# Fourteen elementwise shares and nineteen weight splits taken from GpSimd and given to VectorE

## The chip, the core and the metric

The kernel runs on one core of a Trainium2 chip. A core has TensorE for matrix products, VectorE, ScalarE and GpSimd for elementwise work, and SyncE, whose queue issues nearly all of this kernel's transfers between HBM and the core's memories SBUF and PSUM. The metric is the device time of one execution in microseconds (us); lower is better.

## The reference, cut to what matters

A token sequence of 256 rows and 1024 columns in float32 runs through three layers. Each layer begins with an RMS norm, a wide input product, a mixer and an output product; the first two layers also have an MLP with a squared ReLU.

```python
x = x + rmsnorm(even_mixer(rmsnorm(x, g[0]), ...), g[1])      # layer 0
x = x + rmsnorm(sq_relu_mlp(rmsnorm(x, g[2]), w1, w2), g[3])
...                                                           # layer 1: odd_mixer and a second MLP
h = rmsnorm_2(x, norm_g) * (1 + scale) + shift                # layer 2: scale, shift and gate from silu(c) @ w_ada + b_ada
merged = sigmoid(m_attn) * y_attn + sigmoid(m_conv) * y_conv
return rmsnorm_2(x + gate * (merged @ w_out), final_g)
```

`even_mixer` joins a gated linear recurrence over 4 heads (`hgrn2_scan`, its output normed per head, times a learned gain, times `silu(hgate)`) and a retention over 4 heads whose queries and keys are turned by `rope`, `x1 * cos - x2 * sin` and `x2 * cos + x1 * sin`. `odd_mixer` is an mLSTM behind a short convolution. Layer 2 joins causal attention with a bias by distance and a gated short convolution.

## The kernel before, in words

All weights are read once from HBM, 512 KB at a time, into one of five `raw` buffers (`RB`). TensorE multiplies in a format with fewer bits than float32, so each such unit is split into two parts that add up to it: ScalarE copies `raw` into the high part (`A`, L261), and a subtraction makes the low part from `raw` and the high part. Both lie in one of eight `u` buffers (`NU`). Each product then takes three passes: high by high, low by high and high by low. The activations are split in the same way: `to_act` transposes a normed row on TensorE, ScalarE copies the high part out of PSUM, VectorE subtracts for the low part. The operations are written through small helpers: `tt` is an elementwise operation on two tensors (L265 in the profile), `stt` one with a scalar between (L276), `A` one of ScalarE (L261), `mm` a product (L292), `tr` a transpose (L296).

The instruction streams of the engines are ordered when the program is built. `Sched` keeps an estimate of when each engine is through with what it was given, by a cost for each instruction and the tiles it reads and writes; `sc.E["p"]` (also `sc.t`) is TensorE's estimate, `"v"`, `"a"` and `"g"` are those of VectorE, ScalarE and GpSimd. The products of weights are a list `prog` of steps, each with a cost, and so each weight unit has a time at which it is due. After each product `sc.run` resumes side jobs (norm chains, scans, gates, which are generators) whose estimated time has come, and then calls `pump`. `pump` issues loads as long as a `raw` buffer is free, and splits units ahead of need, up to eight. A unit that is due within `LEAD` (7000 ns) is split as soon as its load is nearly there. One that is due later waits, if its load isn't there, if ScalarE is over 800 ns ahead of TensorE, or if the earlier of VectorE and GpSimd (GpSimd with 1100 ns on top) is over 500 ns ahead. `need` splits whatever a product needs at once. Each engine then executes its stream in the order that resulted, and semaphores make it wait for what it reads or overwrites.

In `emit_split` (L375) the low part goes to GpSimd where its estimated end there is 200 ns (`POOL_BIAS`) or more ahead of that on VectorE:

```python
fv, fg = max(sc.E["v"], hi_t) + 1137.0, max(sc.E["g"], hi_t) + 2220.0
tt(u[:, 1, :], t, u[:, 0, :].bitcast(F32), ALU.subtract, "g" if fg < fv + POOL_BIAS else "v")
```

Three more places give `tt` the engine `"g"`, GpSimd:

- `post` (L570) ends a norm chain. For each half of the 128 rows' columns VectorE multiplies the product by the row's scale and a gain, and `x` is added to: the first half on GpSimd, the second on VectorE. `pre` then takes the squares of both halves on ScalarE, VectorE scales, and `to_act` transposes and splits.
- `rope_evac` (L859): three products on VectorE, then their sum on GpSimd; TensorE transposes the sum.
- `ev_first` (L702): the gate `silu(hgate)` times the learned gain `ghg`, the same for all rows. `ghg` is loaded by `small_loads` (L665), which is called in the same step, one after the scan's `masks`.

GpSimd also does memsets. The blocks `stagA` and `out_stag` take the 256 tokens in two halves of 128, so that the norm chain of one half can run beside the products of the other; `blockA` and `blockB` take all tokens together. Between one output product and the next input product lies a norm chain; such places are called transitions below. While `hgrn` (the scan of layer 0) runs as a side job, TensorE multiplies for the retention.

Of the kernel before, what the change touches and what calls it, by code (L numbers as in the profile page):

```python
# [10 lines left out]
F32 = mybir.dt.float32  # L11
# [3 lines left out]
ALU = mybir.AluOpType  # L15
# [16 lines left out]
LEAD = 7000.0  # L32
POOL_BIAS = -200.0

# [13 lines left out]
class Sched:  # L48
    """Orders the instruction streams. It keeps an estimate of when each engine is through
    with what it was given and when each part of a tile was last written and read, and  # L50
    resumes side jobs (generators) when what they issued last should have finished."""

# [70 lines left out]
    def reuse(self, tag, bufs, ap):  # L123
        """A new tile in the place of the bufs-th last one of its tag."""
        ring = self.ring.setdefault(tag, [])
        ring.append(ap)
        if len(ring) > bufs:
            old = ring.pop(0).tensor.name
            acc = self.W.get(old, []) + self.R.get(old, [])
            self.W[ap.tensor.name] = [(0, 1 << 20, t, w) for l, h, t, w in acc]  # L130
# [39 lines left out]
class Act:  # L170
    """An activation, split into two float32r parts that add up to it exactly,
    features on partitions; lay 'tk': [128, 2, K, 128], 'kt': [128, K, 256]."""

# [30 lines left out]
def tile_model(ctx: ExitStack, tc: tile.TileContext, I: dict, out: bass.AP, stop=None):  # L204
# [36 lines left out]

    # ---------------------------------------------------------- instructions
    def fs(ap):
# [57 lines left out]
    def bc(ap2, n):  # L301
        """[128, m] -> [128, n, m], the same for each of n."""
        return ap2[:, None, :].to_broadcast([ap2.shape[0], n, ap2.shape[1]])
# [4 lines left out]

    # ------------------------------------------------------------ constants
    x = cpool.tile([128, 2, D], F32, name="x")  # L310
# [26 lines left out]

    # ----------------------------------------------------- streams of weights
    units = []
# [35 lines left out]
    def emit_split():  # L375
        k = st["split"]
        kind, val = order[k]
        t = raws.pop(k)
        if kind == "w":
            u = pool.tile([128, 2, 1024], F32R, tag="u", bufs=NU, name=nm("u_"))  # L380
            if len(st["free"]) >= st["nu"] - NU + 1 > 0:
                sc.W[u.tensor.name] = [(0, 2048, st["free"][st["nu"] - NU], "p")]
            st["nu"] += 1
            A(u[:, 0, :], t)
            hi_t = sc.E["a"] + sc.OTHER
            fv, fg = max(sc.E["v"], hi_t) + 1137.0, max(sc.E["g"], hi_t) + 2220.0
            tt(u[:, 1, :], t, u[:, 0, :].bitcast(F32), ALU.subtract, "g" if fg < fv + POOL_BIAS else "v")
            tiles[val] = u
            st["live"] += 1
        else:  # L390
            val[1](t)
        st["done"].append(max(sc.E["v"], sc.E["a"] + 1300.0))
        st["split"] += 1

    def pump():
        while True:
# [8 lines left out]
            if order[k][0] == "w" and due[order[k][1]] - st["at"] > LEAD:  # L405
                if st["arrive"][k] > sc.t + 300 or sc.E["a"] > sc.t + 800 or \
                        min(sc.E["v"], sc.E["g"] + 1100.0) > sc.t + 500:
                    return
# [34 lines left out]

    # ------------------------------------------------------ weight products
    def mmA(ps, act, T, kt, u, off, start, stop_):
# [18 lines left out]
    def blockA(w, c0, act, evac, alloc=None):  # L464
        """512 columns, tokens on partitions; evac({T: bank})."""
        us = units1(w, c0)
# [14 lines left out]
    def stagA(wcs, act, evac, before=None):  # L481
        """Two blocks of 512 columns: both for one half of the tokens, then both for the other."""
        us = [units1(w, c) for w, c in wcs]
# [17 lines left out]
    def blockB(w, c0, act, evac, alloc=None, nk=8):  # L501
        """512 columns as four groups of 128 partitions, tokens along the row; evac([bank, bank])."""
        us = units1(w, c0, 0, nk)
# [14 lines left out]

    # ------------------------------------------------------------ norm chains
    def junk():  # L520
        return pool.tile([128, 512], F32, tag="junk", bufs=1, name=nm("junk_"))

    class Stat:
        """Sum of squares over a row of 1024 in two halves, and 1/sqrt(mean + eps)."""

# [16 lines left out]
    def to_act(src, act, T, k0, n):  # L542
        """src [128 tokens, n*128] -> its transpose in act (k0.. of half T)."""
        pt = axb()
# [25 lines left out]
    def post(T, st_, yb, g):  # L570
        """x += rmsnorm(y) * g; the first half of y is in st_ already."""
        rs = st_.second(yb[1])
        for h in range(2):
            c = slice(h * 512, h * 512 + 512)
            t = s2()
            stt(t, yb[h], rs, g[:, c], ALU.mult, ALU.mult)
            tt(x[:, T, c], x[:, T, c], t, ALU.add, "g" if h == 0 else "v")
        yield
# [6 lines left out]
    class Stage:  # L585
        """Jobs that bring h for one stage, half by half."""

# [12 lines left out]
    def row_order(n):  # L600
        """(half of the columns, unit): unit by unit, but the last ones by halves of the columns,
        so that the first half is there early."""
        return ([(h, j) for j in range(n - TAIL) for h in range(2)]
                + [(h, j) for h in range(2) for j in range(n - TAIL, n)])

    def out_stag(us, act_of, nxt, gpost, gpre, shift=None, ybanks=None, first=True):
        """The last eight rows-units of an out-product: half T of the tokens at a time,
        the norms of one half under the products of the other."""
        n = len(us)
# [22 lines left out]

    # =============================================================== layer 0
    w_ev = I["ev_w_in"][0]
# [3 lines left out]
    def setup():  # L638
# [5 lines left out]
        for h in range(2):  # L644
            c = slice(h * 512, h * 512 + 512)
            A(g_z[0][0:1, c], g_row[:, c])
            tt(g_z[1][0:1, c], g_row[:, c], g_z[0][0:1, c].bitcast(F32), ALU.subtract)
        # work that raises TensorE's clock while the first loads are under way
        warm = axb()
        for i in range(WARM):  # L650
            nc.tensor.matmul(warm.rearrange("p (a c) -> p a c", a=4), ones, bc(ones, 4), start=True, stop=True)
            if i == WARM - AFTER - 1:
                # the first norm's gain, the same for all tokens
                G["g", 0, 0] = [axb(), axb()]
# [25 lines left out]
    def vec_job():  # L680
        pt = axb()
        tr(pt[:, 0:84], vec_in, ident[0:84, 0:84])
        A(vec, pt[:, 0:84])
        # lower bound: softmax over the three rows, row 0
        e = small(16)
# [14 lines left out]

    # ---- hgrn: values and gate
    def ev_first(T, b, ps):  # L702
# [8 lines left out]
        else:  # L711
# [3 lines left out]
            tt(s_.rearrange("p (h c) -> p h c", h=4), s_.rearrange("p (h c) -> p h c", h=4), bc(ghg, 4),  # L715
               ALU.mult, "g")
            E1["g", T] = s_
# [35 lines left out]
    def hgrn():  # L753
# [20 lines left out]
        for l in range(8):  # L774
# [3 lines left out]
            if l == 5:  # L778
                # per 128: the upper halves of both blocks, then the lower ones
                for g in range(2):  # L780
# [65 lines left out]

    # ---- retention
    def ret_consts():
# [10 lines left out]
    def rope_evac(key):  # L859
        def evac(ps):  # L860
            def job():
                dst = s4()
                E1[key] = dst
                for T in range(2):
# [6 lines left out]
                    tt(b3[:, :, 64:128], p3[:, :, 0:64], bc(sn[:, 64:128], 4), ALU.mult)  # L871
                    tt(m1, m1, m2, ALU.add, "g")
                    yield
# [47 lines left out]
    def ret_out(b):  # L921
        """Two heads: out and norm, half by half; left unscaled by the gate."""
        def job():
# [53 lines left out]

    # ---- out-product of layer 0's mixer
    def gains(keys):
# [24 lines left out]

    # ================================================================== MLP
    def mlp(l, stage, nxt, gpost, gpre, shift=None, ada=None):
# [69 lines left out]

    # =============================================================== layer 1
    w_od = I["od_w_in"][0]
# [29 lines left out]
    def od_gates():  # L1108
# [7 lines left out]
        def job():  # L1116
# [4 lines left out]
            ts(ig, ig, 15.0, None, ALU.mult)  # L1121
            # log sigmoid(z) = min(z, 0) - log1p(exp(-|z|))
            ts(z, z, 15.0, None, ALU.mult)
# [18 lines left out]
            yield  # L1142
            # -M, the same for all partitions, by way of DRAM
            nm4 = s4()
# [11 lines left out]
            yield  # L1156
            # columns: a, exp(-m) for each half of the tokens
            pc = axb()
# [8 lines left out]
            while not sj.done:  # L1167
                yield 200.0
            # W[s, t] = exp(a_s - M_t) for s <= t
            for i in range(2):  # L1170
# [37 lines left out]
    def od_qk(key, o, scale):  # L1208
        """Convolution and silu, two heads at a time."""
        def evac(ps):  # L1210
# [37 lines left out]
    def mix(i):  # L1248
        """Two heads' scores, weighted."""
        yield  # L1250
# [17 lines left out]
    def mix_out(T, i):  # L1268
        """Two heads' out and norm for one half of the tokens, left ungated."""
        yield  # L1270
# [72 lines left out]

    # ---- modulation of the last layer, from w_ada as it streams by
    MOD = {}
# [53 lines left out]
    
    # =============================================================== layer 2  # L1400
    w_in = I["w_in_2"][0]
# [114 lines left out]

    # ---- short convolution, channels on partitions
    def conv_half(b):
# [146 lines left out]

    # ------------------------------------------------- order of the loads, run
    if stop is not None:
# [45 lines left out]
def _constants():  # L1713
    """Tables that depend on the shapes alone."""
    f4 = np.float32
# [56 lines left out]
```

## Time and profile before

| | |
|---|---|
| time, median of 3 runs | 1014.26 us (1013.77 to 1014.43) |
| span of the profiled execution | 1010.5 us |
| time that lies around the span, by the median | 3.8 us |
| TensorE, matrix products | 973.0 us busy, 96% of the span |
| VectorE | 679.1 us busy, 67%, 852 instructions |
| ScalarE | 540.8 us busy, 54% |
| GpSimd | 71.5 us busy, 7%, 44 instructions |
| transfers | 191 MB, 189 GB/s over the span |

The profiler's page gives the span from the first to the last instruction of one execution; its whole time isn't recorded apart from the runs, so the median stands for it. Busy time counts an instruction from its start to its end, and an engine that stands within an instruction counts as busy. A bracket behind a row gives the idle time of that engine just before, and what ended it.

### The profile page before, as it was taken

To read this page: it belongs to the slowest core of one execution; us is meant where nothing else is said; L and a number is where in the kernel's file an instruction comes from. 1 tells how busy PE (TensorE), PEld (TensorE's weight loads), DVE (VectorE), ACT (ScalarE), POOL (GpSimd) and SP (SyncE) were. 2 spreads that over 40 slices of the span, in tenths; PEclk is the share of its full clock that TensorE was granted. 3 is DMA by queue.
4 is the path that set the end of the run, shared out by engine and by line. 5 is a ranking of instruction groups with operands and counts; after the bars stand their busy time and mean duration, and the time that the engine had idled before them with its cause. 6 is when DMAs were issued, how large, how long until landed. Compare 5 with 4: busy or idle time off the path is not lost.

```text
span 1010.5 us, 15542 instructions
## 1 busy us (share of the span) xinstructions
PE 973.0 (96%) x6168; PEld 878.1 (87%) x6168; DVE 679.1 (67%) x852; ACT 540.8 (54%) x772; POOL 71.5 (7%) x44
## 2 busy tenths in 40 slices
PE   8999999999999999998999999999949999999997
PEld 6988888799999988977799999878949999999995
DVE  6869774865555556976988886676416677547564
ACT  7753664755444457766665444475316546444443
POOL 0212100200000020201100010010000010001000
PEclk9999999999999999999999999999979999999999
DMA  9762535565666646524789887546467445665531
GB/s 322 251 199 84 183 111 186 167 208 188 229 177 196 190 148 215 185 71 141 232 318 324 303 298 239 162 128 233 94 165 257 148 126 167 209 188 170 191 120 42
DMA packets 85100, 191.09 MB, mean 189 GB/s; under 512 B 7072, under 2 KB 10400, under 8 KB 85028
## 3 DMA queue, kind: packets, MB, share of 16 engines
q1 hardware_dynamic: 84740, 189.58, 58.4%
q8 instruction: 48, 0.79, 0.3%
q10 hardware_dynamic: 288, 0.52, 0.1%
q14 instruction: 24, 0.20, 0.0%
HBM read 187.46 MB, written 2.63 MB: 188 GB/s over the span
## 4 chain that ended last, share of the span: by engine, by line
PE 37%; issue 7%; DMA 5%; DVE 2%; ACT 1%; POOL 0%; SPq 0%; DVEq 0%; ACTq 0%; POOLq 0%
PE mm L292 31%; PE ax L292 6%; DMA scr<-s 3%; DMA raw<-in_w_in_dram 1%; DVE u L265 1%; PE ax L296 1%; DVE s L265 1%; DMA raw<-in_mlp_w_dram 1%; ACT u L261 0%; POOL u L265 0%; DVE s L276 0%; ACT s L261 0%; DVE x L265 0%; ACT junk L261 0%; POOL x L265 0%
## 5 line engine op out<-in xcount | busy, mean ns | idle before, releaser
L265 DVE TENSOR_TENSOR u<-raw,u 128x1024 fp32r<-128x1024 f32 x297 | 367.3, 1249 | 219.5 <-ACT u L261 216.9
L261 ACT ACTIVATE u<-raw 128x1024 fp32r<-128x1024 f32 x316 | 330.5, 1056 | 285.7 <-PE mm L292 139.3
L292 PE MATMUL mm<-u,a 128*128 128x512 f32 x1968 | 470.4, 395 | 4.6 <-DVE a L265 3.2
L292 PEld LDWEIGHTS mm<-u,a 128*128 128x128 f32 x1968 | 366.3, 189 | 81.8 <-DVE a L265 4.6
L292 PE MATMUL mm<-a,u 128*128 128x256 f32 x2496 | 307.2, 285 | 13.9 <-ACT s L261 13.9
L292 PEld LDWEIGHTS mm<-a,u 128*128 128x128 f32 x2496 | 303.0, 193 | 15.4 <-ACT s L261 14.1
L292 PEld LDWEIGHTS ax<-a,u 128*128 128x128 f32 x1152 | 139.9, 192 | 1.0
L292 PE MATMUL ax<-a,u 128*128 128x256 f32 x1152 | 140.6, 283 | 0.0
L265 POOL TENSOR_TENSOR u<-raw,u 128x1024 fp32r<-128x1024 f32 x19 | 47.7, 2512 | 474.8 <-ACT u L261 331.3
L280 DVE RECIPROCAL sm<-sm 128x1 f32<-128x1 f32 (+2 forms) x43 | 7.0, 163 | 54.6 <-ACT sm L261 45.8
L261 ACT ACTIVATE s<-mm 128x512 f32<-128x512 f32 x64 | 35.6, 588 | 10.2 <-PE mm L292 9.9
L296 PE MATMUL ax<-ident,s 128*128 128x128 f32 (+1 forms) x196 | 30.3, 274 | 9.9 <-DVE s L265 7.1
L261 ACT ACTIVATE a<-s 128x512 fp32r<-128x512 f32 (+1 forms) x37 | 23.9, 645 | 28.9 <-DVE s L265 28.1
L296 PEld LDWEIGHTS ax<-ident,s 128*128 128x128 f32 (+1 forms) x196 | 22.7, 141 | 18.3 <-issue 7.0
L261 ACT ACTIVATE s<-ax 128x512 f32<-128x512 f32 (+1 forms) x43 | 24.3, 565 | 25.3 <-PE ax L296 13.8
L261 ACT ACT_TABLE_LOAD x27 | 34.6, 1283 | 2.1 <-DVE lbv L265 0.9
L265 DVE TENSOR_TENSOR s<-mm,s 128x512 f32<-128x512 f32 (+1 forms) x46 | 27.7, 637 | 10.7 <-PE mm L292 6.8
L265 POOL TENSOR_TENSOR x<-x,s 128x512 f32<-128x512 f32 x8 | 10.3, 1290 | 335.7 <-DVE s L276 335.7
L261 ACT ACTIVATE a<-ax 128x512 fp32r<-128x512 f32 x38 | 22.2, 592 | 21.0 <-PE ax L296 20.4
L265 DVE TENSOR_TENSOR a<-s,a 128x512 fp32r<-128x512 f32 x36 | 24.9, 693 | 10.9 <-ACT a L261 8.4
L265 DVE TENSOR_TENSOR s<-s,s 128x512 f32<-128x512 f32 (+4 forms) x38 | 30.4, 803 | 2.6 <-ACT s L261 1.9
L292 PE MATMUL ax<-s,s 128*128 128x256 f32 (+2 forms) x156 | 30.6, 337 | 1.0 <-ACT s L261 0.9
(101 smaller groups left out, 436.6 us busy)
## 6 DMA issues: line engine op xcount, KB each, us to landing
raw<-in_mlp_w_dram SPq DMA_DIRECT2D x128, 512.0 KB
raw<-in_w_in_dram SPq DMA_DIRECT2D x80, 512.0 KB
raw<-in_ev_w_in_dram SPq DMA_DIRECT2D x40, 512.0 KB
raw<-in_od_w_in_dram SPq DMA_DIRECT2D x24, 512.0 KB
raw<-in_w_ada_dram SPq DMA_DIRECT2D x24, 512.0 KB
raw<-in_ev_w_out_dram SPq DMA_DIRECT2D x12, 512.0 KB
s<-in_norm_g_dram SPq DMA_DIRECT2D x8, 512.0 KB
raw<-in_od_w_out_dram SPq DMA_DIRECT2D x8, 512.0 KB
```

Of the source, the lines that this page charges most:

```text
L261: nc.scalar.activation(o, i, f, **kw)
L265: (nc.vector if e == "v" else nc.gpsimd).tensor_tensor(out=o, in0=a, in1=b, op=op)
L280: nc.vector.reciprocal(o, i)
L292: nc.tensor.matmul(o, l, r, start=start, stop=stop_)
L296: nc.tensor.transpose(o, i, idt)
```

## The change

The argument `"g"` is dropped in `post`, `rope_evac` and `ev_first`, so that `tt` takes its default, VectorE. In `emit_split` the choice and its constant go, and every low part is made on VectorE. `pump`, which held back an early split by the earlier of two engines, now looks at VectorE alone. GpSimd keeps its memsets. Comments and docstrings are also removed, which issues no instruction.

```diff
-POOL_BIAS = -200.0
...
             A(u[:, 0, :], t)
-            hi_t = sc.E["a"] + sc.OTHER
-            fv, fg = max(sc.E["v"], hi_t) + 1137.0, max(sc.E["g"], hi_t) + 2220.0
-            tt(u[:, 1, :], t, u[:, 0, :].bitcast(F32), ALU.subtract, "g" if fg < fv + POOL_BIAS else "v")
+            tt(u[:, 1, :], t, u[:, 0, :].bitcast(F32), ALU.subtract)
...
                 if st["arrive"][k] > sc.t + 300 or sc.E["a"] > sc.t + 800 or \
-                        min(sc.E["v"], sc.E["g"] + 1100.0) > sc.t + 500:
+                        sc.E["v"] > sc.t + 500:
                     return
...
             stt(t, yb[h], rs, g[:, c], ALU.mult, ALU.mult)
-            tt(x[:, T, c], x[:, T, c], t, ALU.add, "g" if h == 0 else "v")
+            tt(x[:, T, c], x[:, T, c], t, ALU.add)
...
             tt(s_.rearrange("p (h c) -> p h c", h=4), s_.rearrange("p (h c) -> p h c", h=4), bc(ghg, 4),
-               ALU.mult, "g")
+               ALU.mult)
...
                     tt(b3[:, :, 64:128], p3[:, :, 0:64], bc(sn[:, 64:128], 4), ALU.mult)
-                    tt(m1, m1, m2, ALU.add, "g")
+                    tt(m1, m1, m2, ALU.add)
```

## Rows read from the trace of the kernel before

**Rows 1.** The page's first part: busy us, share of the span, instructions.

```profile
PE 973.0 (96%) x6168; PEld 878.1 (87%) x6168; DVE 679.1 (67%) x852; ACT 540.8 (54%) x772; POOL 71.5 (7%) x44
```

**Rows 2.** TensorE's timeline: start, us, instructions, idle before and its end.

```profile
75.14 0.66 PE L296 MATMUL ax<-ident,s 128*128 128x128 f32 x4 [1.45 <-POOL s L265]
...
189.83 9.63 PE L292 MATMUL mm<-u,a 128*128 128x512 f32 x34 [1.83 <-DVE a L265]
...
449.30 0.66 PE L296 MATMUL ax<-ident,s 128*128 128x128 f32 x4 [1.97 <-DVE s L265]
462.75 0.63 PE L296 MATMUL ax<-ident,s 128*128 128x128 f32 x4 [3.42 <-DVE s L265]
487.37 8.91 PE L292 MATMUL mm<-u,a 128*128 128x512 f32 x38 [1.35 <-DVE a L265]
...
670.15 0.65 PE L296 MATMUL ax<-ident,s 128*128 128x128 f32 x4 [1.72 <-DVE s L265]
758.15 4.52 PE L292 MATMUL mm<-a,u 128*128 128x256 f32 x24 [13.93 <-ACT s L261]
```

**Rows 3.** Busy time by stretch: PE, PEld, DVE, ACT, POOL, PEclk, DMA share, GB/s.

```profile
80.00:120.00 40.00, 40.00 (x237) 34.03 (x237) 38.41 (x49) 19.73 (x24) 9.84 (x6) 1.00 0.44 144
...
190.00:195.00 5.00, 5.00 (x16) 3.95 (x17) 4.93 (x7) 2.28 (x6) 1.29 (x1) 0.66 0.85 293
...
450.00:455.00 5.00, 5.00 (x16) 3.98 (x15) 3.35 (x10) 3.00 (x7) 0.00 (x0) 0.66 0.32 92
```

**Rows 4.** GpSimd's groups by form: busy us, mean ns of one, idle before.

```profile
L265 POOL TENSOR_TENSOR u<-raw,u 128x1024 fp32r<-128x1024 f32 x19 | 47.7, 2512 | 474.8 <-ACT u L261 331.3 <-DVE u L265 143.5
L265 POOL TENSOR_TENSOR x<-x,s 128x512 f32<-128x512 f32 x8 | 10.3, 1290 | 335.7 <-DVE s L276 335.7
L265 POOL TENSOR_TENSOR s<-s,s 128x512 f32<-128x512 f32 x4 | 5.1, 1280 | 13.9 <-DVE s L265 13.9
L265 POOL TENSOR_TENSOR s<-s,ghg 128x512 f32<-128x512 f32 x2 | 4.4, 2192 | 31.6 <-DMA ghg<-in_ev_hg_norm_g_dram 25.7 <-DVE s L265 5.9
```

**Rows 5.** Timeline of the first 48 us, around the gate product with `ghg`.

```profile
23.50 0.69 DVE L265 TENSOR_TENSOR s<-mm,s 128x512 f32<-128x512 f32 x1 [1.41 <-ACT s L261]
...
25.32 3.95 DVE L265 TENSOR_TENSOR u<-raw,u 128x1024 fp32r<-128x1024 f32 x3 [1.13 <-ACT u L261]
...
28.24 2.18 POOL L265 TENSOR_TENSOR s<-s,ghg 128x512 f32<-128x512 f32 x1 [25.67 <-DMA ghg<-in_ev_hg_norm_g_dram]
...
33.71 14.55 PE L292 MATMUL mm<-a,u 128*128 128x256 f32 x120
...
34.46 1.23 DVE L265 TENSOR_TENSOR u<-raw,u 128x1024 fp32r<-128x1024 f32 x1 [0.78 <-ACT u L261]
```

**Rows 6.** Timeline, three stretches: VectorE alone and beside a split of GpSimd.

```profile
180.76 2.35 DVE L265 TENSOR_TENSOR u<-raw,u 128x1024 fp32r<-128x1024 f32 x2
...
184.61 4.56 DVE L265 TENSOR_TENSOR u<-raw,u 128x1024 fp32r<-128x1024 f32 x2
...
443.30 0.16 DVE L265 TENSOR_TENSOR sm<-sm 128x2 f32<-128x2 f32 x1
...
445.61 2.12 DVE L265 TENSOR_TENSOR sm<-sm 128x2 f32<-128x2 f32 x1
...
667.17 2.37 POOL L265 TENSOR_TENSOR u<-raw,u 128x1024 fp32r<-128x1024 f32 x1 [3.05 <-ACT u L261]
667.23 2.86 DVE L265 TENSOR_TENSOR s<-s,s 128x512 f32<-128x512 f32 x1
```

**Rows 7.** Timeline: low parts out of PSUM beside a split of GpSimd.

```profile
371.63 2.50 POOL L265 TENSOR_TENSOR u<-raw,u 128x1024 fp32r<-128x1024 f32 x1 [6.92 <-ACT u L261]
...
371.78 1.28 DVE L265 TENSOR_TENSOR a<-ax,a 128x512 fp32r<-128x512 f32 x2
```

**Rows 8.** Timeline: VectorE's part of one `post`, at 178 us.

```profile
178.17 1.41 DVE L276 SCALAR_TENSOR_TENSOR s<-mm,sm,s 128x512 f32<-128x512 f32 x2
...
179.61 1.23 DVE L265 TENSOR_TENSOR x<-x,s 128x512 f32<-128x512 f32 x1
```

## The prediction

> **What bounds the kernel now.** I read the page's first part, then TensorE's own waits, then what VectorE and GpSimd do just ahead of each wait. TensorE is busy for 973.0 of 1010.5 us, VectorE for 679.1, GpSimd for 71.5 [rows 1]. So time can be won only where TensorE stands or runs at a lower clock, and lost only where it is made to stand anew. Its longest wait, 13.93 us at 758, ends with a ScalarE copy behind a transfer, and no GpSimd operation lies near it; I leave it as it is. Six shorter waits lie beside GpSimd work: 1.45 us at 75, 1.83 at 190, 1.97 at 449, 3.42 at 463, 1.35 at 487 and 1.72 at 670, in sum 11.7 us [rows 2]. [...]
>
> GpSimd does 19 splits (2.51 us each), 8 residual adds, 4 rope adds and 2 gate products [rows 4]. What these cost VectorE is seen in the durations of VectorE's own instructions. An add of 128x512 takes 0.69 us [rows 5], but the one that starts 0.06 us after a GpSimd split takes 2.86. A product of two columns takes 0.16 us, and 2.12 beside a split. Two splits on VectorE take 2.35 us, and 4.56 beside a third on GpSimd [rows 6]. So VectorE stands for some 2 us. I count this at 15 of the 19 splits; at two it is 0.3 and 1.4 us, at two nothing. Where the VectorE work takes one operand from PSUM it isn't held: two low parts take 1.28 us beside a GpSimd split, 0.64 each [rows 7].
>
> **The change, part by part.** *Splits.* Each becomes a VectorE instruction of 2.35 / 2 = 1.18 us [rows 6]. Added: 19 x 1.18 = 22.4 us. Handed back: 15 x 2.0 = 30 us.
>
> [...]
>
> *The six waits.* If a split keeps its place in the order, VectorE does 1.18 us where it stood for 2, and the chain behind it gains the difference. At 190: 4.56 - 3 x 1.18 = 1.0 us, and as much at 487, where the pattern repeats. At 449: 2.12 - 0.16 - 1.18 = 0.8, and again at 463. At 670: 2.86 - 0.69 - 1.18 = 1.0. At 75 TensorE waits for the rope add itself: 1.28 on GpSimd against 0.69, 0.6 us. Lower bound: 0.6 + 1.0 + 0.8 + 0.8 + 1.0 + 1.0 = 5.2 us. Upper bound: the split moves behind the chain, and the block goes whole, as far as the wait reaches: 1.45 + 1.83 + 1.96 + 1.96 + 1.35 + 1.72 = 10.3. The upper end has a reason in the code: GpSimd was chosen when VectorE's estimate was more than a microsecond ahead, and `pump` now holds an early split back when that estimate is over 500 ns past TensorE's. The lower end has the reason that splits due within 7 us are not held. I take the middle, 7.7.
>
> [...]
>
> *Residual adds.* Now two multiply-adds (1.41 us) run on VectorE, GpSimd adds the first half, and VectorE's own add takes 1.23 for 0.69 because it is held [rows 8]. After: 1.41 + 2 x 0.69 = 2.8 us for 1.41 + 1.23 = 2.64. The chain ends 0.15 us later, but its first half is ready earlier, and ScalarE's squares of that half come off the end. I count nothing; what covers it is the product of the other half of the tokens. Added: 8 x 0.69 = 5.5 us; handed back 8 x 0.54 = 4.3.
>
> *Rope adds and gate products.* 6 x 0.69 = 4.1 us on VectorE, in stretches where TensorE has work queued. Rope's adds now stand ahead of the scan's masks. Should three of these 14 adds meet a chain with no cover, that is 3 x 0.69 = 2.1 us. I charge it.
>
> *A new wait.* The first gate product needs `ghg`, whose transfer lands at 28.24; GpSimd waits for it harmlessly. VectorE would stand from about 24.2 to 28.24, and behind it the three splits now at 25.32 start at 28.93, 3.6 us late; behind these the softmax of the lower bound, and with it ScalarE's next splits [rows 5]. TensorE asks for the first of these units at 33.71 and takes 24 x 14.55 / 120 = 2.9 us for each. The fourth, now ready at 34.46 + 1.23 = 35.7, would be ready at 39.3 and is wanted at 33.71 + 3 x 2.9 = 42.4. Cover: 3.1 us, so I count nothing; with the cover gone it is up to 3.6 us.
>
> *Transfers.* None is moved. A raw buffer is free once its low part is made, so a load behind a former GpSimd split can start 1.3 us sooner; those behind the new wait up to 3.6 us later, within the same cover.
>
> Sum: 7.7 + 1.7 - 2.1 = 7.3 us. The span goes from 1010.5 to 1003.2. What lies around it, 1014.3 - 1010.5 = 3.8 us by the median of the runs, is untouched: 1007.0 us. VectorE's busy time becomes 679.1 + 22.4 + 5.5 + 4.1 - 30 - 4.3 = 677 us, not 711.
>
> **The rivals.** *The first 120 us eat the gain.* From 80 to 120 VectorE is busy for 38.41 of 40 us [rows 3]. Three splits and two rope adds there add 3 x 1.18 + 2 x 0.69 = 4.9 us where 1.6 are free: 3.3 us late if nothing is handed back. With the 3.6 us of the `ghg` wait that makes 6.9, and the time 1007.0 + 6.9 = 1013.9: no change. For it: VectorE fills that stretch as no other. Against: two of its three splits hold VectorE up, so most of the 4.9 comes back, and the scan's own end isn't wanted until the mixer's output product. It decides once TensorE uses up the units split ahead.
>
> [...]
>
> *Splits come too late: slower.* `pump` used to look at the earlier of VectorE and GpSimd, and with GpSimd idle it hardly ever held a split back; now VectorE's estimate alone holds it until 7 us before it is due. At four transitions into blocks that take tokens half by half (190, 384, 487, 670) a unit of 1024 columns feeds six products at first, 6 x 8.91 / 38 = 1.4 us [rows 2], so eight units go in 11.3 us. In that time VectorE has the other half's chain to do, 1.41 + 1.38 + 1.41 + 1.28 = 5.5 us [rows 7, 8], and room for (11.3 - 5.5) / 1.18 = 4.9 splits. So three to four units must be ready beforehand. From the first one missing, each costs 1.2 us: two at each of four places are 9.4 us. The gains at 190, 487 and 670 go (3.0 of 5.2), 2.2 stay, and I leave the clock out: 1014.3 - 2.2 + 9.4 = 1021.5; with one missing 1016.8. I put it at 1018. Against it: 7 us at 1.4 us a unit is five units, more than four.
>
> *GpSimd's shares go, but each split lands exactly where it was, and the clock stays.* Then 5.2 - 2.1 = 3.1 us: 1011.2, faster still, the weak end of my forecast.
>
> **How the numbers follow.** Forecast, the weak end with it: 0.70, from 1014.3 - 10.3 - 3.4 = 1000.6 to 1011.2. First 120 us: 0.18, 1013.9. Late splits: 0.12, 1018. The predicted time is 1007.0. The range runs from 1001, the upper bound of the gain, to 1015, past the second case; the third is left out, with a little at either end. A measurement of this kernel can tell 0.2%, 2 us, from no change: faster than 1012.2 0.70, between 0.18, slower than 1016.3 0.12.
>
> **What would show it.** GpSimd keeps 11 memsets and some 4 us. VectorE has 885 instructions and 670 to 685 us; at 700 or more, little was handed back. A sum over 128x512 beside what was a split takes 0.69 us, two splits 2.35. The waits at 75, 190, 449, 463, 487 and 670 are shorter by 5 us together at least, and TensorE's clock is 1.00 around 190 or around 450. VectorE stands some 4 us for `ghg` near 24 us, and TensorE doesn't stand at 34 to 45. The wait of 13.9 us behind the bias transfer stays. I am wrong if TensorE waits for a weight unit made by VectorE at the transitions, or between 34 and 120 us.

## The result, and the profile of the changed kernel

The changed kernel takes 1005.62 us (median of four runs, 1003.08 to 1006.18), beside 1014.28 for the kernel before (1013.77 to 1014.43). The ratio is 0.9909, with a 95% interval of 0.9895 to 0.9923: faster by 8.7 us. In a later group of runs the same pair gave 1006.09 and 1014.41, ratio 0.9922 (0.9900 to 0.9945). The profiled execution took 1005.89 us, with a span of 1004.1.

The page's first part, which answers to [rows 1], shows where the elementwise time went:

```profile
PE 972.5 (97%) x6168; PEld 879.0 (88%) x6168; DVE 669.7 (67%) x885; ACT 540.4 (54%) x772; POOL 4.1 (0%) x11
```

VectorE has 33 instructions more and is busy 9.4 us less. GpSimd falls from 71.5 us to 4.1, eleven memsets. TensorE does the same work (972.5 us for 973.0), so that of the 6.4 us by which the two profiled spans differ 5.9 are time in which TensorE no longer stands. VectorE's groups by form (busy us, mean ns of one, idle before) show how 33 more can take less time:

```profile
L264 DVE TENSOR_TENSOR u<-raw,u 128x1024 fp32r<-128x1024 f32 x316 | 380.2, 1222 | 214.1 <-ACT u L260 211.9 <-PE mm L291 0.7
L264 DVE TENSOR_TENSOR s<-s,s 128x512 f32<-128x512 f32 x26 | 17.8, 688 | 0.5
L264 DVE TENSOR_TENSOR x<-x,s 128x512 f32<-128x512 f32 x20 | 13.8, 692 | 0.7
```

In the same view of the kernel before, a split on VectorE took 1249 ns on average over 297, the sum `s<-s,s` 785 over 22, and the residual add 1064 over 12. Now both kinds of add take 0.69 us on average, and so do the second adds of `post`, of which [rows 8] show one at 1.23. The rows of VectorE's timeline that answer to [rows 6] are the three splits at 184, the two-column product at 441, which took 2.12 us before, and the sum at 662; the one at 187 answers to [rows 7].

```profile
178.92 0.74 DVE L275 SCALAR_TENSOR_TENSOR s<-mm,sm,s 128x512 f32<-128x512 f32 x1
179.69 0.69 DVE L264 TENSOR_TENSOR x<-x,s 128x512 f32<-128x512 f32 x1
...
184.10 3.49 DVE L264 TENSOR_TENSOR u<-raw,u 128x1024 fp32r<-128x1024 f32 x3
187.50 1.28 DVE L264 TENSOR_TENSOR a<-ax,a 128x512 fp32r<-128x512 f32 x2
...
441.46 0.16 DVE L264 TENSOR_TENSOR sm<-sm 128x2 f32<-128x2 f32 x1
...
662.28 0.69 DVE L264 TENSOR_TENSOR s<-s,s 128x512 f32<-128x512 f32 x1
```

Three splits now take 3.49 us on VectorE alone, where two took 4.56 while GpSimd made the third.

TensorE's timeline, the rows of the transitions with the idle time before each, answers to [rows 2]:

```profile
188.25 8.26 PE L291 MATMUL mm<-u,a 128*128 128x512 f32 x35 [1.04 <-DVE a L264]
...
457.11 1.94 PE L295 MATMUL ax<-ident,s 128*128 128x128 f32 x8 [2.87 <-DVE s L264]
482.31 10.93 PE L291 MATMUL mm<-u,a 128*128 128x512 f32 x45 [1.28 <-ACT a L260]
679.51 0.66 PE L295 MATMUL ax<-ident,s 128*128 128x128 f32 x4 [0.34 <-DVE s L264]
752.51 4.98 PE L291 MATMUL mm<-a,u 128*128 128x256 f32 x24 [14.18 <-ACT s L260]
```

The waits at 75, 449 and 670 are gone, those at 190, 463 and 487 are 1.04, 2.87 and 1.28 us. With a new 0.34 at 679 that makes 5.5 us for 11.7: 6.2 less. What is left at 457 has a new form: the two sums that TensorE needs stand behind two splits in VectorE's queue.

```profile
454.01 2.35 DVE L264 TENSOR_TENSOR u<-raw,u 128x1024 fp32r<-128x1024 f32 x2
456.28 1.29 DVE L264 TENSOR_TENSOR s<-s,s 128x512 f32<-128x512 f32 x2
```

Busy time by stretch (PE, PEld, DVE, ACT, POOL, PEclk, DMA share, GB/s) answers to [rows 3]:

```profile
80.00:100.00 20.00, 20.00 (x127) 17.34 (x126) 18.40 (x28) 8.54 (x11) 0.00 (x0) 1.00 0.12 31
100.00:120.00 20.00, 20.00 (x118) 16.91 (x116) 15.30 (x22) 9.21 (x13) 0.00 (x0) 1.00 0.52 160
190.00:195.00 5.00, 5.00 (x24) 4.13 (x23) 4.90 (x6) 2.37 (x5) 0.00 (x0) 1.00 0.62 211
...
455.00:460.00 5.00, 2.89 (x11) 2.73 (x12) 5.00 (x7) 3.39 (x5) 0.00 (x0) 0.64 0.72 234
460.00:465.00 5.00, 5.00 (x17) 3.90 (x17) 1.03 (x2) 0.00 (x0) 0.00 (x0) 0.68 0.91 330
```

From 80 to 120 us VectorE is busy for 33.7 us and no longer for 38.41. The clock at 190 is 1.00 now, but the ten microseconds from 455 have 0.64 and 0.68.

The head answers to [rows 5]: VectorE stands 3.85 us for `ghg`, and TensorE runs on through 34 us.

```profile
24.52 0.69 DVE L264 TENSOR_TENSOR s<-mm,s 128x512 f32<-128x512 f32 x1 [1.44 <-ACT s L260]
29.06 0.69 DVE L264 TENSOR_TENSOR s<-s,ghg 128x512 f32<-128x512 f32 x1 [3.85 <-DMA ghg<-in_ev_hg_norm_g_dram]
...
34.74 15.52 PE L291 MATMUL mm<-a,u 128*128 128x256 f32 x128
```

### The profile page after: what moved, and what is told of

Read it like the earlier page. It is cut to its first block, busy times and chain, and to the rows that moved or that the text cites. A ratio compares the mean times of both kernels' runs of the same rounds, so it can differ in the third digit from the quotient of the medians.

```text
span 1004.1 us, 15488 instructions
## 1 busy us (share of the span) xinstructions
PE 972.5 (97%) x6168; PEld 879.0 (88%) x6168; DVE 669.7 (67%) x885; ACT 540.4 (54%) x772; POOL 4.1 (0%) x11
## 4 chain that ended last, share of the span: by engine, by line
PE 82%; DVE 7%; DMA 5%; ACT 3%; issue 2%; SPq 0%; DVEq 0%; ACTq 0%
PE mm L291 62%; PE ax L291 18%; DMA scr<-s 3%; DVE u L264 3%; DVE s L275 2%; PE ax L295 2%; DMA raw<-in_w_in_dram 1%; DMA x<-in_x_dram 1%; DVE s L264 1%; ACT u L260 1%; ACT junk L260 1%; ACT L260 1%; ACT s L260 1%; DVE x L264 1%; SPq L306 0%
## 5 line engine op out<-in xcount | busy, mean ns | idle before, releaser
L264 DVE TENSOR_TENSOR u<-raw,u 128x1024 fp32r<-128x1024 f32 x316 | 380.2, 1222 | 214.1 <-ACT u L260 211.9
L264 DVE TENSOR_TENSOR a<-ax,a 128x512 fp32r<-128x512 f32 x38 | 25.6, 687 | 7.1 <-ACT a L260 7.1
L275 DVE SCALAR_TENSOR_TENSOR s<-raw,silc,s 128x1024 f32<-128x1024 f32 x21 | 26.9, 1280 | 0.3
```

What stands on the lines that cost most here:

```text
L264: (nc.vector if e == "v" else nc.gpsimd).tensor_tensor(out=o, in0=a, in1=b, op=op)
L275: nc.vector.scalar_tensor_tensor(out=o, in0=a, scalar=s, in1=b, op0=op0, op1=op1, **kw)
```

## The experiments

The theory was the prediction's: GpSimd's instructions hold VectorE's up, and the change gives that time back. The rivals: it is the new order of the streams that gains (the planner sees one engine less), or the new clause in `pump`, or the missing latency of GpSimd's slow results.

**One part at a time.** First the splits and the clause in `pump` alone, with the fourteen small shares left on GpSimd; then the small shares alone, with the choice in `emit_split` and the clause of before.

```diff
# splits alone, from the kernel before
... (the two lines that set fv and fg go)
-            tt(u[:, 1, :], t, u[:, 0, :].bitcast(F32), ALU.subtract, "g" if fg < fv + POOL_BIAS else "v")
+            tt(u[:, 1, :], t, u[:, 0, :].bitcast(F32), ALU.subtract)
...
-                        min(sc.E["v"], sc.E["g"] + 1100.0) > sc.t + 500:
+                        sc.E["v"] > sc.t + 500:
# small shares alone, from the kernel before
-            tt(x[:, T, c], x[:, T, c], t, ALU.add, "g" if h == 0 else "v")
+            tt(x[:, T, c], x[:, T, c], t, ALU.add)
... (and the same in ev_first and rope_evac)
```

> Only the weight splits and the hold in pump are changed; the residual adds, rope adds and gate products stay on GpSimd. Theory A (a GpSimd operation that reads SBUF holds up VectorE work with two SBUF operands, and the splits are the long ones): most of the gain is here, 1006 to 1009 us, span 1004 to 1006, VectorE's split mean back at 1.22 us, its residual add still about 1.06. Theory C (the fourteen small shares stood in the norm and rope chains): little gain, 1012 us or more. Theory D (about 2 us of the gain lie around the span and hang on GpSimd doing any operation that reads SBUF): time minus span stays near 3.8 us, not 1.8.

> Only the residual adds, rope adds and gate products go to VectorE; splits are shared out as before. Theory A: 1012 to 1014 us, at most the 1.4 us wait at 75 us goes, the waits near 449, 463, 487 and 670 stay. Theory C: 1007 to 1009 us. Theory D: time minus span stays near 3.8 us.

The splits alone, with their clause, give 1003.25 us, ratio 0.9892 (0.9878 to 0.9905): the whole gain. The small shares alone make the kernel slower than before: 1028.75, ratio 1.0143 (1.0125 to 1.0160). GpSimd's groups by form show what else changed: with its small shares gone the planner believes GpSimd free, and hands it 32 splits for 19.

```profile
L265 POOL TENSOR_TENSOR u<-raw,u 128x1024 fp32r<-128x1024 f32 x32 | 82.9, 2591 | 856.2 <-ACT u L261 730.2 <-DVE s L276 101.9 <-DMA vec_in<-in_conv_w_dram 24.1
```

So with thirteen more splits on GpSimd and 14 small operations fewer the kernel takes 14.5 us more; VectorE is busy for 687.2 us, 8.1 more than before, although thirteen splits of 1.18 us fewer outweigh 14 small operations more. This run doesn't price the small shares by themselves.

**The order kept, the engine changed.** The planner of before is left whole, with GpSimd's estimate, so that all streams keep their order; only the instruction is issued on the other engine.

```diff
-        (nc.vector if e == "v" else nc.gpsimd).tensor_tensor(out=o, in0=a, in1=b, op=op)
+        nc.vector.tensor_tensor(out=o, in0=a, in1=b, op=op)
```

> The planner decides exactly as in the kernel before, so that every engine but these two keeps its order, but each instruction that it gives to GpSimd is issued on VectorE at the same place. Theory A: VectorE stands no longer, and the waits shrink by the difference of some 0.8 to 1.0 us at five places and 0.6 at one, my lower bound: 5 us, and 2 around the span: 1006.5 to 1009 us. Rival B (the gain comes from the planner's new order, in which pump holds early splits back and the norm chains go first): within 2 us of before but for the time around the span, 1011.5 us or more.

1006.19 us, ratio 0.9917 (0.9903 to 0.9932), within 0.6 us of the changed kernel. The new order isn't needed for the gain; the engine alone brings it.

**GpSimd work put back into the changed kernel.** Every sixteenth split is executed on GpSimd, while the planner books it for VectorE, so that the order stays.

```diff
+            if k % 16 == 8:
+                sc.op("v", 1137.0, [u[:, 1, :]], [t, u[:, 0, :].bitcast(F32)])
+                nc.gpsimd.tensor_tensor(out=u[:, 1, :], in0=t, in1=u[:, 0, :].bitcast(F32), op=ALU.subtract)
+            else:
+                tt(u[:, 1, :], t, u[:, 0, :].bitcast(F32), ALU.subtract)
```

> The changed kernel, its planner and the order of every stream untouched, but the low part of every sixteenth unit (20 of 316) is made by GpSimd in place of VectorE; the planner still charges VectorE for it. Theory A (GpSimd's read of SBUF holds VectorE up): VectorE instructions beside these 20 last some 2 us longer, and the time rises by 3 to 9 us over the 1005.6 of the changed kernel, to 1008.5 to 1015. Rival B (only the order of the streams matters): 1004 to 1007 us.

1010.28 us, ratio 0.9957 (0.9941 to 0.9973): with twenty splits on GpSimd 4.4 us of the gain are left by the ratio, about half (the kernel before took 1015.40 in this group of runs). Is it that they arrive late (2.67 us for 1.22), or that they hold VectorE up? In the next two kernels all splits stay on VectorE, and GpSimd does work whose result nobody reads: twenty adds that read 768 columns of a high part, or twenty times a one-column add and three memsets, which only write.

```diff
+    idle = cpool.tile([128, 768], mybir.dt.bfloat16, name="idle")
...
+            if k % 16 == 8:
+                h_ = u[:, 0, 0:768].bitcast(F32)
+                nc.gpsimd.tensor_tensor(out=idle, in0=h_, in1=h_, op=ALU.add)
# the other kernel, in place of the last line
+                nc.gpsimd.tensor_tensor(out=idle[:, 0:1], in0=h_[:, 0:1], in1=h_[:, 0:1], op=ALU.add)
+                for _ in range(3):
+                    nc.gpsimd.memset(idle, 0.0)
```

> The changed kernel with 20 more GpSimd instructions, at every sixteenth unit: each adds 768 columns of the unit's high part to themselves, into a tile that nobody reads. VectorE keeps all splits. Theory A: VectorE is held for up to the 1.9 us that each lasts, and the time rises by 2 to 7 us, to 1007.5 to 1012.5. Rival E (what costs is that a split made by GpSimd is ready 1.3 us later, not that VectorE stands): 1004 to 1007 us, as without them.

> As the run with the added additions, but GpSimd only writes: at every sixteenth unit one addition of a single column, which waits for the unit's high part, and then three memsets of the same unread tile. Theory A in its strict form (GpSimd's reads hold up VectorE's second operand from SBUF, its writes don't): 1004 to 1007 us, and no VectorE instruction longer than its kind. If any GpSimd work holds VectorE up: the rise of the additions again, 2 to 7 us.

The adds give 1011.89 us, ratio 0.9964 (0.9948 to 0.9979); the memsets, in the same group of runs, 1005.95, ratio 0.9916 (0.9901 to 0.9930). The memsets leave the changed kernel's gain whole, and the adds cost 5.9 us more than they. The groups by form of the kernel with the adds, GpSimd's and VectorE's, then those of the kernel with the memsets:

```profile
L388 POOL TENSOR_TENSOR idle<-u 128x768 bf16<-128x768 f32 x20 | 43.0, 2152 | 907.7 <-ACT u L260 907.7
L264 DVE TENSOR_TENSOR u<-raw,u 128x1024 fp32r<-128x1024 f32 x316 | 392.7, 1264 | 202.3 <-ACT u L260 200.9
```

```profile
L390 POOL MEMSET idle<- 128x768 bf16 x60 | 44.7, 744 | 3.5
L264 DVE TENSOR_TENSOR u<-raw,u 128x1024 fp32r<-128x1024 f32 x316 | 380.3, 1222 | 214.0 <-ACT u L260 212.5
```

GpSimd is as long busy in both, 43.0 and 44.7 us. Beside reads VectorE's split rises from 1222 to 1264 ns on average, beside writes it stays at 1222; all of VectorE's work together is busy for 687.1 us beside the twenty reads and for 670.1 beside the writes. No instruction waits for one of the added adds by the trace, so what they cost isn't a `u` buffer that they keep too long. And TensorE stands again where it had stood before (timeline of the kernel with the adds):

```profile
188.89 9.84 PE L291 MATMUL mm<-u,a 128*128 128x512 f32 x35 [2.31 <-DVE a L264]
...
433.70 2.11 PE L291 MATMUL mm<-u,a 128*128 128x512 f32 x8 [1.53 <-DVE u L264]
```

That is the cause of the gain shown from both sides: an otherwise unused GpSimd instruction costs time here if it reads wide operands from SBUF (5.9 us for twenty), and none that can be seen if it writes (ratio 0.9916 with sixty memsets and twenty one-column adds, 0.9909 for the changed kernel). With the twenty splits on GpSimd the low parts `a<-s,a`, both operands in SBUF, took 933 ns on average for 693 in the changed kernel, and `a<-ax,a`, one operand in PSUM, 686 for 687, which agrees with [rows 7].

**The clause in `pump`.** It came with the change, and the prediction saw in it mainly a danger. Three kernels: the changed one without it; the kernel before with it and nothing else; the splits-alone kernel with a stricter bound.

```diff
# changed kernel, no hold by VectorE
-                if st["arrive"][k] > sc.t + 300 or sc.E["a"] > sc.t + 800 or \
-                        sc.E["v"] > sc.t + 500:
+                if st["arrive"][k] > sc.t + 300 or sc.E["a"] > sc.t + 800:
# kernel before, hold by VectorE alone
-                        min(sc.E["v"], sc.E["g"] + 1100.0) > sc.t + 500:
+                        sc.E["v"] > sc.t + 500:
# splits alone, stricter
-                        sc.E["v"] > sc.t + 500:
+                        sc.E["v"] > sc.t - 1000:
```

> The changed kernel without the clause of pump that holds an early split back by VectorE's estimate; loads and ScalarE still hold it. Theory A: the hold matters little, 1004 to 1008 us. Rival B: without it the splits stand before the norm chains on VectorE, and 3 us or more of the gain go: 1008.5 us or more, with longer waits near 188, 457, 482 and 664.

> The kernel before with one edit: pump holds an early split back by VectorE's estimate alone, as in the changed kernel. GpSimd keeps 16 splits and its fourteen small shares. Theory A (contention is what the change removes): most of the loss stays, 1009 to 1014 us. Rival B (the hold is what the change brings): 1003 to 1008 us.

> The splits-only kernel with a stricter hold: an early split waits unless VectorE's estimate is 1000 ns or more behind TensorE's (before: until 500 ns ahead). If what the hold brings grows with it, the waits in front of the norm chains shrink further: 1000 to 1002.5 us. If splits come too late then, TensorE waits for units made by VectorE: 1004 us or more.

Without a hold by VectorE: 1018.66 us, ratio 1.0049 (1.0035 to 1.0064), slower than before although GpSimd does nothing but its memsets. In the profiled executions TensorE stands for 40.6 us, for 31.6 in the changed kernel, and is busy for 978.1, for 972.5. These 5.6 us, more than a third of the loss, go with a lower granted clock: 0.980 on average for 0.989, and 0.58 from 195 to 200 us and 0.61 from 465 to 470, where the changed kernel has 1.00. The clause alone: 1012.18, ratio 0.9976 (0.9964 to 0.9988), with 16 splits still on GpSimd: 2.4 us by the ratio, 3.2 by the medians. The stricter one: 1012.11, ratio 0.9983 (0.9965 to 1.0001), 9 us behind the looser one. VectorE's timeline without the hold, and TensorE's wait that follows:

```profile
180.85 0.69 DVE L264 TENSOR_TENSOR x<-x,s 128x512 f32<-128x512 f32 x1
181.46 4.62 DVE L264 TENSOR_TENSOR u<-raw,u 128x1024 fp32r<-128x1024 f32 x4
186.00 0.15 DVE L279 RECIPROCAL sm<-sm 128x1 f32<-128x1 f32 x1
...
192.77 1.28 DVE L264 TENSOR_TENSOR a<-ax,a 128x512 fp32r<-128x512 f32 x2
...
193.51 5.49 PE L291 MATMUL mm<-u,a 128*128 128x512 f32 x12 [3.70 <-DVE a L264]
```

Four splits stand between the residual add and the reciprocal that the norm chain goes on with, and the low parts that TensorE waits for come at 192.77, behind the other half's `post` as well. In the kernel with the old planner and the old clause, all on VectorE, two splits stand there:

```profile
181.66 2.35 DVE L265 TENSOR_TENSOR u<-raw,u 128x1024 fp32r<-128x1024 f32 x2
183.93 0.15 DVE L280 RECIPROCAL sm<-sm 128x1 f32<-128x1 f32 x1
```

So the old clause did hold splits back, too. By its code, it lets one pass while GpSimd's estimate lies in the past, and that one's own cost then holds the next; this reading was only argued. Too strict a hold fails at the other end: TensorE waits for a weight unit (its timeline in the stricter kernel; 0.32 us in the looser one). That wait is only part of the 9 us. In the profiled executions TensorE stands 1.9 us longer than in the looser kernel (33.2 for 31.3) and is busy 4.1 us longer (973.8 for 969.7).

```profile
430.17 3.51 PE L292 MATMUL mm<-u,a 128*128 128x512 f32 x14 [2.64 <-DVE u L265]
```

**The gate products on GpSimd again.** This prices VectorE's stand of 3.85 us for `ghg`.

```diff
-               ALU.mult)
+               ALU.mult, "g")
```

> The changed kernel with the two gate products given back to GpSimd, so that GpSimd and not VectorE waits for the gain's transfer near 25 us. My account has that wait covered: within 2 us of the changed kernel, 1004 to 1007.5 us. If it isn't covered, up to 3.6 us less: 1001 to 1003.

> The changed kernel once more, beside the others of this call: 1005.6 us within 1.5. The splits-only kernel had 1003.25 with a ratio to before whose interval overlaps with this one's; if the fourteen small shares cost time on VectorE, the ratio here is above 0.9892 with an interval that leaves it out.

1005.90 us, beside 1006.09 for the changed kernel in the same group of runs: no difference. The stand is covered, as the prediction had it.

**Both bias transfers on another queue.** The longest wait, 14.18 us, ends behind a transfer of bias rows. The splits-alone kernel with its two issues moved from SyncE's queue to GpSimd's:

```diff
-        load(scr, bm[0:8, None, :].to_broadcast([8, 128, 384]))
+        load(scr, bm[0:8, None, :].to_broadcast([8, 128, 384]), nc.gpsimd)
... (and nc.gpsimd for the load of the bias tile that follows)
```

> The splits-only kernel (GpSimd keeps its fourteen small shares), and the two transfers of the attention bias are issued by GpSimd's queue, which now has time, in place of SyncE's, where the loads of weights stand behind them. If the wait of 14 us near 750 comes from that queue alone, it goes, and with it the stretch at the lower clock behind it: 1003 - 14 - 3 = 986 us, 984 to 991. If VectorE, which must wait for the bias in its own order, becomes the next to stand there: 993 to 1001.

1001.61 us (1001.08 to 1002.57), ratio 0.9881 (0.9855 to 0.9907), the lowest median of all, but only 1.6 us below the splits alone, whose interval it overlaps, and just above what was expected at most. TensorE's waits there are 7.14 and 3.44 us (its timeline) for 14.13 and 1.21 in the splits-alone kernel, 4.8 us less, while the first transfer takes 34.7 us to land (the view of transfers: KB, us):

```profile
743.93 5.49 PE L292 MATMUL mm<-a,u 128*128 128x256 f32 x24 [7.14 <-ACT s L261]
752.87 1.65 PE L292 MATMUL ax<-s,s 128*128 128x128 f32 x4 [3.44 <-ACT s L261]
```

```profile
scr<-s POOLq DMA_DIRECT2D x1, 1536.0 KB, 34.7
```

Weight loads are no longer queued behind the bias, but both halves of the wait still end with ScalarE's copies. Why these are still late wasn't settled. Most of what the waits gave went elsewhere: in the profiled executions TensorE stands for 26.9 us, for 31.3, but is busy for 973.9, for 969.7.

## Why the prediction was right, and where its terms were off

**The mechanism** stands: GpSimd's reads hold VectorE's two-operand instructions up, its splits from 1222 to 1264 ns on average beside twenty adds. It was read off 15 of 19 splits and is shown now by the order-keeping kernel, the adds that nobody reads and the memsets.

**VectorE's busy time** was forecast at 677 us (670 to 685) and is 669.7, just below that. Added were 32 us, as counted; handed back were 679.1 + 32 - 669.7 = 41.4, not 34.3. The splits-alone kernel divides this. The splits handed back 679.1 + 22.4 - 668.3 = 33.2 us, not 30: 2.0 was a low average, and the two that hold VectorE for 0.3 and 1.4 us were left out. The small operations handed back the other 8.2, not 4.3: the count took only the eight adds of `post` as held. The gate products hold VectorE, too, as a row beside the first of them shows (before, then after):

```profile
29.19 1.26 DVE L265 TENSOR_TENSOR sm<-vec 128x4 f32<-128x4 f32 x1
```

```profile
30.81 0.15 DVE L264 TENSOR_TENSOR sm<-vec 128x4 f32<-128x4 f32 x1
```

**The six waits** were to give 7.7 us and gave 6.2, within the bounds of 5.2 to 10.3. The upper bound's reason, that splits move behind the chain, came true only in part: at 184 and at 454 splits still stand ahead of it.

**The clock** was to give 1.7 us, an estimate for one of the two stretches at 0.66 in [rows 3], 5 x 0.34: 16 products run in five microseconds there, and 24 at a clock of 1.00 (190 to 195 us, the changed kernel). No run shows that term by itself; what the changed kernel showed in its place is a gain of nearly nothing, 0.5 us of TensorE's busy time. The stretches at 190 and 450 went, but 455 to 465 lost nearly as much as both had cost, 3.0 of 3.4 us: from the end of the wait at 457.11 the clock was 0.50 up to 460, 2.89 x 0.50 = 1.4 us, and behind it 5 x 0.32 = 1.6. In the splits-alone kernel the same wait of 2.87 us, at 456.33, is followed by a clock of 1.00:

```profile
455.00:460.00 5.00, 3.67 (x20) 3.10 (x21) 5.00 (x7) 2.55 (x4) 0.00 (x0) 1.00 0.71 229
460.00:465.00 5.00, 5.00 (x24) 4.14 (x23) 0.26 (x1) 0.55 (x2) 0.00 (x0) 1.00 0.92 367
```

24 products in the second five microseconds, where the changed kernel does 17. A term of this kind should have been put down as a spread, not as a gain.

**The three small adds**, charged at 2.1 us, can't be found as such: no new wait behind one of them, and VectorE has room from 80 to 120. The splits-alone kernel is 2.4 us quicker, and its interval (0.9878 to 0.9905) just meets that of the changed kernel (0.9895 to 0.9923). The changed kernel's second ratio, 0.9922, has an interval from 0.9900 that leaves 0.9892 out, which was to be the sign that the small shares cost time on VectorE. But the profiled executions put 2.8 of their 3.1 us on TensorE's busy time (972.5 for 969.7), so on the clock stretch above; the waits of 1.04 and 1.28 at 188 and 482 are nearly gone there (0.28 at 478), and others have come in their place. Whether the small shares themselves cost anything on VectorE, or the clock fell otherwise, stays open.

**Around the span** the prediction put 3.8 us, by setting the profiled execution against the median. The runs list span and time together: 1005.89 with 1004.1 after, 1011.13 with 1009.4 before; it is 1.7 to 2.3 us in all of them. So the profiled execution of before was some 2 us quicker than its median; what made the others longer no trace shows. That hid 2 us of the gain: spans differ by 6.4 us, medians by 8.7. With 1.8 in its place the sum was 1010.5 + 1.8 - 7.3 = 1005.0. That the 7.3 us lie so near the 6.4 of the spans is partly luck: waits and clock were put 1.5 and 1.7 us too high, and the charge of 2.1 us for the small adds, which no row shows, took most of that back.

**The rivals.** The first 120 us didn't eat the gain: 33.7 us busy of 40, and no wait of TensorE over 0.3 us between 20 and 120. Late splits hardly came at 500 ns (0.31 us at 429) but did with a bound 1500 ns stricter, 2.64 us at 430 in a kernel 9 us slower: the rival was real, and the chosen bound nearly clear of it. What the prediction got wrong is the hold itself. It says that the old clause "hardly ever held a split back", and it took the new one for a reason of the upper bound and for a risk. The runs show that without any hold by VectorE the relocation loses 4.4 us against before, while with the old clause it gains 8, and that the new clause by itself gains 2.4.

## What to carry to other kernels

Before giving a second engine a share, subtract what its instruction does to the first: here a GpSimd split spares VectorE 1.18 us and holds it up for some 2, which shows in the trace as one form of instruction with two durations (0.69 and 2.86 us for one sum). A planner that adds up estimates without that price hands over work at a loss, and the less else the second engine has to do the more it hands over (32 splits for 19). When work moves to the engine of a critical chain, bound how far ahead of its need it may be queued there, and try that bound on both sides: too loose lost 13 us here, too strict 9.

## What the runs showed of the hardware

Memsets on GpSimd cost VectorE nothing here: with 60 of 744 ns its splits took 1222 ns as without, and the time changed by 0.3 us, within the spread. Twenty reads of as long together kept it busy for 17.4 us more. The granted clock after a wait isn't set by the length of that wait alone: the same 2.87 us near 457, ended by the same sum, was followed by 0.64 and 0.68 in the changed kernel, by 1.00 and 1.00 in the splits-alone kernel, and by these in another execution of the changed kernel, which costs 3.0 us, nothing, and 5 x 0.25 + 5 x 0.09 = 1.7 us. Part of the spread between executions lies there:

```profile
455.00:460.00 5.00, 2.80 (x12) 2.47 (x13) 5.00 (x7) 3.47 (x5) 0.00 (x0) 0.75 0.70 225
460.00:465.00 5.00, 5.00 (x22) 4.09 (x21) 1.13 (x2) 0.00 (x0) 0.00 (x0) 0.91 0.91 326
```
